# Masking a chunk's matrices as they leave PSUM, in the recurrence of a two-layer encoder: one VectorE instruction in place of a ScalarE copy and a GpSimd product

## The chip, the cores and the metric

The kernel runs on one core of one Trainium2 chip. The metric is the time of one execution on the device in microseconds (us), the median of several runs. The core's engines work in parallel, each through its own instructions in order: TensorE (PE in the profile, with PEld for its weight loads), VectorE (DVE), ScalarE (ACT), GpSimd (POOL) and the queue SP, which here issues nearly all DMAs. Matmul results land in PSUM, a small memory of eight banks per partition; everything else on the chip lies in SBUF.

## The reference: what is computed

A trunk of two layers on 1024 tokens of width 1024, all in float32. Layer 0 mixes tokens by dilated and windowed attention, layer 1 by a bidirectional recurrence; each layer ends with a squared-ReLU MLP of width 4096. The change lies in the recurrence of layer 1. For each of 16 heads (64 wide) and each of two directions the reference runs, token by token:

```python
def step(state, inp):
    r_t, w_t, k_t, v_t, kk_t, a_t = inp
    sa = jnp.einsum('bhvk,bhk->bhv', state, -kk_t)
    state = (state * w_t[:, :, None, :] + sa[..., None] * (kk_t * a_t)[:, :, None, :]
             + v_t[..., None] * k_t[:, :, None, :])
    return state, jnp.einsum('bhvk,bhk->bhv', state, r_t)
```

## The kernel before

The program is one stream: attention, MLP, the projections of the recurrence, the recurrence (`rwkv_scan`), the second MLP. The order of instructions on each engine is laid out at build time by the framework's planner from a simulated timeline with estimated durations (`schedule_with_timeline_sim=True`), within the data dependences and the priorities that the program gives. A change of an instruction's engine can therefore also change the order of its neighbours.

The recurrence is computed in chunks of 64 tokens. Heads are taken in eight batches (`Batch`), each with four steps (`G` counts all 32), and a step holds four pairs of heads and chunks for each of two directions `d`. Four generators do the work of a step:

- `prep` (lines 1240 to 1288) loads `x` and `rk`, takes exponentials on ScalarE (L1250, L1251), writes `zr` on VectorE (L1254, L1256) and `bk` half on VectorE (L1261) and half on GpSimd (L1262). Then, for `j` of 0 and 1, four matmuls (L1268) put a 128x512 block of the chunk's matrices into a PSUM tile, and the block goes to `af` in SBUF, multiplied by the triangular mask `amask`. These are the two instructions of the change, L1271 and L1272. After that `bk` is transposed (L1280) and copied to `bn` (L1282), and once both directions are done a part of `af` is written to `nd` in DRAM (L1286). `bk` is one buffer, so the next direction's L1261 and L1262 wait for the transposes. The PSUM tiles `A` of L1268 and L1280 come from a ring of two (`psA`).
- `invert` (lines 1290 to 1321) loads a batch's `nd` back as `nb` (L1294) and inverts its triangular blocks by thirty pairs of VectorE instructions, each needing the one before (L1300 and L1302), then sends the inverses through DRAM (`xd`) into `af`.
- `post` (from line 1323) completes the inverses for a step by small matmuls.
- `scan` (from line 1374) carries the states from chunk to chunk, with high priority: matmuls into `c`, evicted by ScalarE as `y` (L1395), the solved values `sv` copied by VectorE for one half (L1398) and by ScalarE for the other (L1399), the new state `h` written by ScalarE (L1407) and the output `ot` (L1418). After each of its pieces `side` puts in a piece of the generators above and of `finish` (group norm and gate, L1435 to L1447).

Before the first `scan` stands a prologue: `prep` of the first four steps, `invert` of the first batch, `post` of the first step, and `prep` of four steps more. From then on `prep` runs eight steps ahead of `scan`.

Of the kernel before, what the change touches and what calls it, by code (L numbers as in the profile page):

```python
# [9 lines left out]
AF = mybir.ActivationFunctionType  # L10
ALU = mybir.AluOpType
# [4 lines left out]
P = 128  # L16
# [9 lines left out]
def fsl(i, n):  # L26
    return slice(i * n, (i + 1) * n)
# [1115 lines left out]
def rwkv_scan(tc, g, ap, dr, yd):  # L1143
# [4 lines left out]
    nc = tc.nc  # L1148
    NS = T // P
    NX = 4 * (65 + 2 * RC)  # L1150
    with ExitStack() as es:
# [24 lines left out]
        consts = {}  # L1176
# [24 lines left out]
        def psa():  # L1201
            return psA.tile([P, 512], F32, tag="A", name="A")
# [7 lines left out]
        def c64(x):  # L1210
            return x.rearrange("p (c t) -> p c t", t=RC)

        def tokens(d, e, n):

            return slice(e * P, (e + n) * P) if d == 0 else slice((NS - e - n) * P, (NS - e) * P)

        def ordered(x, d):

            return (x if d == 0 else x[:, :, ::-1]).rearrange("p q (c t) -> p q c t", t=RC)

        def quad(x):
            return x.rearrange("p (q c) t -> p q c t", q=2)
# [11 lines left out]
        def prep(q, i):  # L1234

            e = 4 * q.half + i
            w = q.slots[i]
            sp = sl[(4 * q.b + i) % NQ]
            w.af = sp.tile([P, 2, 4, 2, P], F32, tag="af", name="af")
            w.zr, w.bn = ([sp.tile([P, 4, 2, RC], F32, tag=f"{n}{d}", name=f"{n}{d}") for d in range(2)] for n in ("zr", "bn"))  # L1240
            w.pc = [sp.tile([P, 4], F32, tag=f"pc{d}", name=f"pc{d}") for d in range(2)]
            for d in range(2):
                x = te.tile([P, NX], F32, tag="x", name="x")
                nc.sync.dma_start(out=x, in_=dr.x[d][q.m][:, e, :])
                rk = te.tile([P, 2, 2, P], F32, tag="rk", name="rk")
                nc.sync.dma_start(out=rk, in_=dr.rk[q.m][:, :, :, tokens(d, e, 1)])
                cs = x[:, 0:260].rearrange("p (q c t) -> p q c t", q=2, c=2)
                a, kd = (x[:, 260:].rearrange("p (q k c t) -> p q k c t", q=2, k=2, c=2)[:, :, k] for k in range(2))
                ipr = te.tile([P, 4, RC], F32, tag="ipr", name="ipr", bufs=1)
                nc.scalar.activation(quad(ipr), cs[..., 1:65], AF.Exp, scale=KAPPA)  # L1250
                nc.scalar.activation(cs, cs, AF.Exp, scale=-KAPPA)  # L1251
                nc.gpsimd.tensor_copy(w.pc[d].rearrange("p (q c) -> p q c", q=2), cs[..., 64])
                zr = w.zr[d]
                nc.vector.tensor_tensor(out=quad(zr[:, :, 0]), in0=cs[..., 0:64], in1=ordered(rk[:, :, 1], d),  # L1254
                                        op=ALU.mult)
                nc.vector.tensor_tensor(out=quad(zr[:, :, 1]), in0=cs[..., 1:65], in1=ordered(rk[:, :, 0], d),  # L1256
                                        op=ALU.mult)

                for j in range(2):
                    rows = fsl(j, 64)  # L1260
                    nc.vector.tensor_tensor(out=quad(bk[rows, :, j, j]), in0=kd[rows], in1=quad(ipr[rows]), op=ALU.mult)  # L1261
                    nc.gpsimd.tensor_tensor(out=quad(bk[rows, :, j, 1 - j]), in0=a[rows], in1=quad(ipr[rows]), op=ALU.mult)  # L1262
                yield

                for j in range(2):
                    ps = psa()
                    for u in range(4):
                        nc.tensor.matmul(ps[:, fsl(u, P)], lhsT=bk[:, u, j].rearrange("p a b -> p (a b)"),  # L1268
                                         rhs=zr[:, u].rearrange("p a b -> p (a b)"), start=True, stop=True)
                    o = w.af[:, d, :, j, :]  # L1270
                    nc.scalar.activation(o, ps.rearrange("p (u t) -> p u t", t=P), AF.Copy)  # L1271
                    nc.gpsimd.tensor_tensor(out=o, in0=o, in1=consts["amask"].unsqueeze(1).to_broadcast([P, 4, P]),  # L1272
                                            op=ALU.mult)
                    yield

                for j in range(2):
                    rows = fsl(j, 64)
                    ps = psa()
                    for u in range(4):
                        nc.tensor.transpose(ps[:, fsl(u, RC)], bk[rows, u, j].rearrange("p a b -> p (a b)"),  # L1280
                                            g.ident[rows, rows])
                    nc.scalar.activation(w.bn[d][:, :, j, :], c64(ps[:, 0:4 * RC]), AF.Copy)  # L1282
                if d == 1:
                    afv = w.af.rearrange("p d c j t -> p (d c) j t")
                    for j in range(2):
                        nc.sync.dma_start(out=q.nd[j, fsl(i, 8)].transpose([1, 0, 2]),  # L1286
                                          in_=afv[fsl(1 - j, 64), :, j, 0:64])
                yield
# [194 lines left out]
        for i in range(4):  # L1483
            b1.add(prep(bs[0], i))
# [7 lines left out]
        for G in range(4, NQ - 1):  # L1492
            if G % 4 == 0:
                bs.append(Batch(G // 4))
            b1.add(prep(bs[G // 4], G % 4))
# [3 lines left out]
        for G in range(4 * NB):  # L1499
# [10 lines left out]
            if g2 < 4 * NB:  # L1510
                if g2 % 4 == 0:
                    bs.append(Batch(g2 // 4))
                b1.add(prep(bs[g2 // 4], g2 % 4))
# [182 lines left out]
```

## Time and profile before

| what | us |
|---|---|
| median of 3 runs | 3607.05 |
| lowest and highest of them | 3602.4 and 3607.34 |
| the profiled execution | 3597.65 |
| its span, first to last instruction | 3595.9 |
| busy of that span: DVE | 2357.0 |
| busy: ACT | 1853.7 |
| busy: POOL | 1778.8 |
| first L1268, last L1268 (start) | 1890.6 and 2657.3 |
| first state copy L1398, last (start) | 2077.4 and 2791.0 |

Times inside the profile are counted from the span's start. The first layer and the projections fill the span up to about 1940; the prologue of the recurrence stands alone until about 2072; the recurrence proper runs to about 2800, and the second layer's output projection and MLP take the rest. A row of the timeline gives start, duration, engine, line, operation, the tile written and the tiles read; in square brackets is the idle time of the engine just before, and what ended it. A row of groups gives busy time and the mean of one instruction after the bar, then the engine's idle time in front of them.

### The profile page before, as it was taken

The numbers are of one execution on the slowest core, as the hardware profiler recorded it, in microseconds if no ns is written. First come the engines' busy times: TensorE is split into PE (matmuls) and PEld (weight loads), VectorE is DVE, ScalarE is ACT, GpSimd is POOL, SyncE is SP. The second block draws the span as 40 slices with busy tenths as digits, with TensorE's granted clock in tenths as the row PEclk, the third lists the DMA queues.
The fourth block names the chain that finished last, engine by engine and source line by source line (L and its number), as shares of the span: only waits on it lengthen the run. The fifth ranks groups of instructions, "written<-read, shape, count | busy, mean of one in ns | idle before, by whom it ended". The sixth has DMA issues, their size and how long they took to land. (4 is left out here: it accounts for less than half of the span.)

```text
span 3595.9 us, 61432 instructions
## 1 busy us (share of the span) xinstructions
PE 3213.8 (89%) x22616; PEld 2618.0 (73%) x22616; DVE 2357.0 (66%) x3917; ACT 1853.7 (52%) x4260; POOL 1778.8 (49%) x1606
## 2 busy tenths in 40 slices
PE   7999998899998897988888689899998989999988
PEld 6788896688876776666556577777776768877776
DVE  3455564654489987977964756766653474449996
ACT  2366564455543336764433366666667455554333
POOL 1000001465578886445557534445431265558887
PEclk9999999899999998999998589889899989999999
DMA  6222215143221323347776445455445322322113
GB/s 205 73 79 78 73 56 170 53 152 117 73 98 59 117 71 118 102 144 234 226 222 200 113 113 129 119 129 136 125 108 155 120 108 104 115 101 104 54 64 118
DMA packets 408203, 425.72 MB, mean 118 GB/s; under 512 B 138155, under 2 KB 321579, under 8 KB 401756
## 3 DMA queue, kind: packets, MB, share of 16 engines
q1 hardware_dynamic: 406716, 417.58, 37.1%
q0 software_dynamic: 1184, 4.20, 0.4%
q8 instruction: 178, 2.92, 0.3%
q14 instruction: 125, 1.02, 0.1%
HBM read 290.83 MB, written 138.20 MB: 119 GB/s over the span
## 5 line engine op out<-in xcount | busy, mean ns | idle before, releaser
L101 PE MATMUL pm<-bhi,lo 128*128 128x512 f32 x840 | 332.1, 398 | 47.8 <-DVE lo L130 47.6
L129 ACT ACTIVATE hi<-x 128x512 fp32r<-128x512 f32 x300 | 189.1, 631 | 340.8 <-DVE x L127 130.3
L130 DVE TENSOR_TENSOR lo<-x,hi 128x512 fp32r<-128x512 f32 x300 | 321.6, 1079 | 65.4 <-ACT hi L129 65.2
L100 PE MATMUL pm<-blo,hi 128*128 128x512 f32 x840 | 331.4, 395 | 8.4 <-POOL blo L130 7.9
L99 PE MATMUL pm<-bhi,hi 128*128 128x512 f32 x840 | 318.0, 395 | 6.2 <-ACT bhi L129 6.2
L127 POOL TENSOR_TENSOR x<-w1r 128x512 f32<-128x512 f32 x160 | 213.9, 1340 | 201.0 <-DVE lo L130 178.1
L130 POOL TENSOR_TENSOR blo<-bx,bhi 128x512 fp32r<-128x512 f32 x138 | 220.2, 1596 | 34.9 <-ACT bhi L129 34.4
L101 PEld LDWEIGHTS pm<-bhi,lo 128*128 128x128 f32 x840 | 157.9, 189 | 100.1 <-DVE lo L130 69.1
L1272 POOL TENSOR_TENSOR af<-af,amask 128x512 f32<-128x512 f32 x128 | 166.1, 1304 | 118.1 <-ACT af L1271 96.4
L905 POOL TENSOR_TENSOR wl<-wr,wh 128x512 fp32r<-128x512 f32 (+2 forms) x144 | 162.5, 1139 | 125.3 <-ACT wh L904 92.5
L1268 PE MATMUL A<-zr,bk 128*128 128x128 f32 x1024 | 181.1, 336 | 44.5 <-DVE bk L1261 40.1
L127 POOL TENSOR_TENSOR bx<-w 128x512 f32<-128x512 f32 x140 | 215.4, 1541 | 9.4
L127 DVE TENSOR_TENSOR x<-h 128x512 f32<-128x512 f32 x140 | 199.4, 1436 | 5.2 <-ACT h L268 2.7
L1268 PEld LDWEIGHTS A<-zr,bk 128*128 128x128 f32 x1024 | 158.5, 238 | 54.8 <-POOL af L1272 21.5
L100 PEld LDWEIGHTS pm<-blo,hi 128*128 128x128 f32 x840 | 158.4, 189 | 50.9 <-POOL blo L130 17.6
L99 PEld LDWEIGHTS pm<-bhi,hi 128*128 128x128 f32 x840 | 159.5, 190 | 39.9 <-ACT bhi L129 7.1
L99 PE MATMUL mm<-xmh,wh 128*128 128x512 f32 x384 | 164.1, 446 | 8.1 <-ACT wh L904 4.9
L1261 DVE TENSOR_TENSOR bk<-x,ipr 64x256 f32<-64x256 f32 x128 | 118.2, 924 | 70.8 <-PE A L1280 62.2
L1398 DVE COPY sv<-c 64x64 f32<-64x64 f32 x256 | 55.2, 226 | 163.9 <-PE c L1397 94.1
L583 ACT ACTIVATE S<-S,mneg 128x256 f32<-128x256 f32 (+2 forms) x256 | 124.6, 499 | 68.2 <-DVE mneg L578 45.3
L335 DVE TENSOR_TENSOR acc<-acc,pm 128x512 f32<-128x512 f32 x256 | 158.1, 674 | 0.0
L886 DVE SCALAR_TENSOR_TENSOR x<-u,mu,x 128x512 f32<-128x512 f32 x192 | 153.3, 831 | 7.2 <-ACT x L884 4.8
(368 smaller groups left out, 9936.7 us busy)
## 6 DMA issues: line engine op xcount, KB each, us to landing
w1r<-in_mlp_w_dram SPq DMA_DIRECT2D x32, 1024.0 KB, 5.6
w<-in_mlp_w_dram SPq DMA_DIRECT2D x32, 1024.0 KB, 5.2
x<-x SPq DMA_DIRECT2D x64, 386.0 KB, 3.5
hd<-h SPq DMA_DIRECT2D x24, 1024.0 KB, 4.2
h<-hd SPq DMA_DIRECT2D x24, 1024.0 KB, 7.8
wr<-in_w_rkv_dram SPq DMA_DIRECT2D x96, 256.0 KB, 2.9
x<-xo SPq DMA_DIRECT2D x32, 512.0 KB, 3.6
rk<-rk SPq DMA_DIRECT2D x64, 256.0 KB, 4.0
```

The source lines that it names most:

```text
L99: nc.tensor.matmul(out, lhsT=ahi, rhs=bhi, start=start, stop=False)
L100: nc.tensor.matmul(out, lhsT=ahi, rhs=blo, start=False, stop=False)
L101: nc.tensor.matmul(out, lhsT=alo, rhs=bhi, start=False, stop=stop)
L127: add.tensor_tensor(out=y, in0=x, in1=blocks[term[2]], op=ALU.add if term[1] == "+" else ALU.subtract)
L129: nc.scalar.activation(hi, x, AF.Copy)
L130: sub.tensor_tensor(out=lo, in0=x, in1=hi, op=ALU.subtract)
L335: dve.tensor_tensor(out=a, in0=a, in1=banks[j], op=ALU.add if sign == "+" else ALU.subtract)
L583: nc.scalar.activation(s[:, :n], s[:, :n], AF.Exp, bias=mneg[:, i:i + 1], scale=-1.0)
L886: nc.vector.scalar_tensor_tensor(out=x, in0=at(2 * i), scalar=mu[:, i, c, kt:kt + 1], in1=x, op0=ALU.mult, op1=ALU.add)
L905: nc.gpsimd.tensor_tensor(out=wlo, in0=wr, in1=whi, op=ALU.subtract)
L1268: nc.tensor.matmul(ps[:, fsl(u, P)], lhsT=bk[:, u, j].rearrange("p a b -> p (a b)"), rhs=zr[:, u].rearrange("p a b -> p (a b)"), start=Tru ...
L1272: nc.gpsimd.tensor_tensor(out=o, in0=o, in1=consts["amask"].unsqueeze(1).to_broadcast([P, 4, P]), op=ALU.mult)
```

## The change

In `prep`, the copy out of PSUM by ScalarE and the product with the mask in place by GpSimd become one product on VectorE, which reads the block from PSUM and the mask from SBUF and writes `af`. It runs once for each `j`, each direction and each of 32 steps: 128 times.

```diff
@@ -1268,9 +1268,8 @@
                         nc.tensor.matmul(ps[:, fsl(u, P)], lhsT=bk[:, u, j].rearrange("p a b -> p (a b)"),
                                          rhs=zr[:, u].rearrange("p a b -> p (a b)"), start=True, stop=True)
                     o = w.af[:, d, :, j, :]
-                    nc.scalar.activation(o, ps.rearrange("p (u t) -> p u t", t=P), AF.Copy)
-                    nc.gpsimd.tensor_tensor(out=o, in0=o, in1=consts["amask"].unsqueeze(1).to_broadcast([P, 4, P]),
-                                            op=ALU.mult)
+                    mask = consts["amask"].unsqueeze(1).to_broadcast([P, 4, P])
+                    nc.vector.tensor_tensor(out=o, in0=ps.rearrange("p (u t) -> p u t", t=P), in1=mask, op=ALU.mult)
                     yield
```

## The prediction, made before the changed kernel was run

> **What bounds the kernel now.** I read the page first, then the busy times by stage, the timeline of the prologue, and the waits of the recurrence. The page has TensorE as the fullest engine, but the share is a mean over stages:
>
> ```profile
> PE 3213.8 (89%) x22616; PEld 2618.0 (73%) x22616; DVE 2357.0 (66%) x3917; ACT 1853.7 (52%) x4260; POOL 1778.8 (49%) x1606
> ```
>
> The busy times by stage (start and end, length, busy of each engine with its count, granted clock, DMA share) part the stretch that holds all of L1271 and L1272 into prologue (first three rows; the second is the inverse of the first batch), recurrence with `prep` beside it, and recurrence alone:
>
> ```profile
> core 0: us, PE busy (x) PEld busy (x) DVE busy (x) ACT busy (x) POOL busy (x), PEclk, DMA share, GB/s
> 1943.00:2003.00 60.00, 40.05 (x224) 35.91 (x224) 37.89 (x38) 24.34 (x55) 43.45 (x52) 0.65 0.57 148
> 2003.00:2053.40 50.40, 30.32 (x152) 27.44 (x153) 46.99 (x86) 15.91 (x36) 27.42 (x32) 0.64 0.36 98
> 2053.40:2100.00 46.60, 30.59 (x444) 26.48 (x444) 27.88 (x75) 21.68 (x66) 12.23 (x17) 0.67 0.41 88
> 2100.00:2660.00 560.00, 521.20 (x7944) 425.83 (x7944) 347.26 (x757) 364.39 (x1204) 266.43 (x322) 0.90 0.51 128
> 2660.00:2830.00 170.00, 147.83 (x2396) 117.55 (x2397) 74.21 (x189) 107.56 (x362) 29.08 (x40) 0.94 0.46 129
> ```
>
> In the prologue nothing is full except DVE during the inverse (46.99 of 50.40); in the recurrence PE is at 521.2 of 560, with 38.8 us idle. So the prologue is a loop bound by latency, and the timeline shows the loop. One turn, in order of time:
>
> ```profile
> 1965.99 0.91 POOL L1262 TENSOR_TENSOR bk<-x,ipr 64x256 f32<-64x256 f32 x1
> 1966.23 3.03 DVE L1261 TENSOR_TENSOR bk<-x,ipr 64x256 f32<-64x256 f32 x2
> 1966.86 1.25 POOL L1272 TENSOR_TENSOR af<-af,amask 128x512 f32<-128x512 f32 x1
> 1968.19 0.79 POOL L1262 TENSOR_TENSOR bk<-x,ipr 64x256 f32<-64x256 f32 x1
> 1968.54 3.40 PE L1268 MATMUL A<-zr,bk 128*128 128x128 f32 x16 [2.34 <-DVE bk L1261]
> 1970.62 0.60 ACT L1271 ACTIVATE af<-A 128x512 f32<-128x512 f32 x1 [0.86 <-PE A L1268]
> 1971.97 0.60 ACT L1271 ACTIVATE af<-A 128x512 f32<-128x512 f32 x1 [0.45 <-PE A L1268]
> 1972.63 0.46 PE L1280 MATMUL A<-ident,bk 64*128 64x64 f32 x4 [0.30 <-ACT af L1271]
> 1973.16 3.03 DVE L1261 TENSOR_TENSOR bk<-x,ipr 64x256 f32<-64x256 f32 x2
> ```
>
> The turn from `bk` to `bk` takes 1973.16 - 1966.23 = 6.93 us: `bk` written, two matmul groups, two evictions, transposes, `bk` again. Of it 3.03 us are the two L1261. They end at 1969.26, 0.28 us after GpSimd's second L1262 (1968.98), and that one stands behind L1272. How long L1261 takes unhindered is seen in the line views (minimum, median, maximum in ns):
>
> ```profile
> L1261 DVE TENSOR_TENSOR bk<-x,ipr x128: 406/829/2931, 1887.9 to 2654.7; 64x256 f32<-64x256 f32 x128
> L1272 POOL TENSOR_TENSOR af<-af,amask x128: 1251/1270/1854, 1899.1 to 2658.7; 128x512 f32<-128x512 f32 x128
> L1271 ACT ACTIVATE af<-A x128: 570/597/619, 1896.9 to 2657.6; 128x512 f32<-128x512 f32 x128
> L335 DVE TENSOR_TENSOR acc<-acc,pm x256: 670/674/677, 1036.4 to 3543.6; 128x512 f32<-128x512 f32 x128
> ```
>
> Two L1261 would be 0.81 us. They are stretched whenever a GpSimd product lies beside them; I read this as GpSimd holding back a VectorE instruction that reads two SBUF tiles. L335, a VectorE product of the same size with one input in PSUM, varies by only 7 ns, though the MLPs keep GpSimd busy beside it. It is the nearest row to the new instruction.
>
> **The change part by part.** Removed: 128 L1271 by 597 ns = 76.4 us of ScalarE, and 128 L1272, 166.1 us of GpSimd by the page. Added: 128 VectorE products; I take L335's 674 ns, so 86.3 us. The mask is read with a repeated axis, which no row shows beside a PSUM input; bounds are 0.6 us (the ScalarE eviction) and 1.27 us (the GpSimd product), and I take the row of the same engine and shape. The dependences stay: matmul, masked block, then the transposes' PSUM tile and the store of `nd`. No DMA is added.
>
> Term A, the turns ahead of the first inverse. In a turn, L1272 goes from between the two L1262. The second L1262 then starts right behind the first and ends at 1966.90 + 0.08 + 0.79 = 1967.77 in place of 1968.98: 1.21 us sooner, and L1261 ends behind it as now. The second eviction costs 0.674 in place of 0.597: +0.08. VectorE is in order, and must now fit mask, `zr` and mask between its `bk`s. `zr` is two instructions of about 0.42 us; between the two masks it fills the time of the second matmul group (1971.97 - 1970.62 = 1.35 us) and 0.67 + 0.84 = 1.51 overhangs by about 0.15. That is -1.21 + 0.08 + 0.15 = -0.98 us a turn. The inverse begins behind the `bk` of 2000.88:
>
> ```profile
> 1945.50 3.02 DVE L1261 TENSOR_TENSOR bk<-x,ipr 64x256 f32<-64x256 f32 x2
> 2000.88 2.15 DVE L1261 TENSOR_TENSOR bk<-x,ipr 64x256 f32<-64x256 f32 x1
> 2002.96 0.70 DVE L1300 TENSOR_TENSOR xtmp<-nb 128x30 f32<-128x30 f32 x1
> 2053.21 0.19 DVE L1302 TENSOR_TENSOR nb<-nb,xtmp 128x30 f32<-128x30 f32 x1
> 1988.91 0.58 SPq L1286 DMA_DIRECT2D nd<-af  x1
> 1991.59 2.11 SPq L1294 DMA_DIRECT2D nb<-nd  x2
> ```
>
> Eight turns lie between those two `bk` (55.4 us / 6.93), so 8 x 0.98 = 7.8, and 1.2 for the last `bk` itself: **A = -9.0**. The data come as early: the last store of `nd` (1988.91) moves with seven turns and with a block that is ready 2 us sooner (0.67 in place of 0.60 and 1.25 in two queues). If the plan puts VectorE's pieces otherwise, A may be -2 (rivals) or at best 9 x 1.25 = -11.
>
> Term B, the inverse itself (2002.96 to 2053.40), where VectorE is full and everything it loses or gains shows:
>
> ```profile
> L1272 POOL TENSOR_TENSOR af<-af,amask 128x512 f32<-128x512 f32 x12 | 15.5, 1288 | 19.8 <-ACT af L1271 14.2 <-issue 5.6
> ```
>
> Twelve L1272 of 15.5 us together stand in VectorE's way there; twelve masks bring 12 x 0.674 = 8.1. **B = -7**, a little under the difference of 7.4. Bounds: -15.5 if the masks fell into VectorE's gaps (there are 3.4 us, so hardly), +8.1 if nothing were given back.
>
> From the end of the inverse to the first state (2053 to 2077) come DMA round trips with few masks: 0. They move forward as a whole.
>
> Term C, the recurrence, 2100 to 2660, with 92 masks. The waits of PE and DVE there (total, times, longest), and the groups:
>
> ```profile
> PE c L1402 <- ACT sv L1399: 26.8, 19, 3.7
> PE c L1410 <- ACT sv L1399: 2.0, 1, 2.0
> DVE sv L1398 <- PE c L1397: 66.6, 46, 5.4
> DVE sv L1398 <- ACT af L1271: 12.8, 5, 4.2
> L1271 ACT ACTIVATE af<-A 128x512 f32<-128x512 f32 x92 | 53.0, 590 | 19.4 <-PE A L1268 10.2 <-PE c L1410 7.0 <-DMA x<-x 0.8
> L1272 POOL TENSOR_TENSOR af<-af,amask 128x512 f32<-128x512 f32 x92 | 119.9, 1312 | 78.3 <-ACT af L1271 64.6 <-DMA af<-xd 6.1 <-ACT ot L1418 6.0
> L1261 DVE TENSOR_TENSOR bk<-x,ipr 64x256 f32<-64x256 f32 x90 | 76.4, 849 | 26.3 <-PE A L1280 21.9 <-ACT y L1395 2.0 <-ACT h L1407 0.5
> ```
>
> Most of PE's 38.8 us of idle time, 28.8 of it, is waiting for the state's copies: `sv` L1399, which follows L1398 on VectorE. ScalarE loses 53.0 us that stood in line with four of the scan's evictions (L1395, L1399, L1407, L1418); VectorE, which has one of them (L1398), gets 92 x 0.674 = 62.0 us. It gets something back: L1261 alone lose 90 x (849 - 406) = 39.9 us there, and L1272 with its 119.9 us is the longest GpSimd work beside them; I put half, 20 us, and as much for the rest of VectorE's two-tile products, both estimates. VectorE ends near 347 + 62 - 40 = 369 of 560 us, not full. The one row that ties a removed instruction to the scan is 12.8 us in which L1398 waited until an L1271 had gone. I take half of it as PE time: **C = -6**, between 0 (PE stays the bound, the waits come back on VectorE) and -28.8 (all these waits go); above zero in the rival.
>
> Sum: -9 - 7 + 0 - 6 = **-22 us**. On the profiled execution (3597.65, of which 3595.9 is span and 1.75 lies around it) that gives 3575.6. The median of the runs shown is 9.4 us above the profiled one; taken from the median, 3607.05 - 22 = **3585 us**.
>
> A rule that speaks against the change: the Trainium skill, page Perfetto Trace Analysis, section Optimizing Scalar/DVE Operations, says that where VectorE is saturated it may make sense to hand work to ScalarE or even GpSimd; this edit does the reverse. By that rule term B would be a loss. The trace bears it out only for that one stretch, and there the row of L1272 speaks for the hindrance being the larger part. It is the last of the rivals.
>
> **The rivals.** *More than forecast.* The state's copies come free: C = -20, sum -36, 3571 us. And the clock: the two matmul groups of a turn took 3.40 us at a low granted clock. Compare these stretches, and a group of eight on the chain of waits later on:
>
> ```profile
> 1910.00:1920.00 10.00, 10.00 (x53) 8.23 (x52) 0.79 (x1) 5.68 (x10) 9.09 (x8) 1.00 0.80 278
> 1990.00:2000.00 10.00, 8.13 (x40) 7.33 (x40) 4.42 (x6) 4.01 (x9) 5.36 (x6) 0.50 0.85 171
> 2429.84 1.09 PE A L1268 x8
> ```
>
> With PE full the clock is 1.00, in the loop with its gap of 2.34 us it is 0.50, and 16 matmul records would take 2.18 us at the speed of the last row. If the shorter turn raised the clock, eight turns would gain 8 x 1.2 = 10 us more. The Trainium skill, page TensorE: Matmul & The Clock Gate, section Part 1 (What's actually happening), has the clock at half after an idle window of about 3.4 us and at full after a busy one. By that rule the loop, whose gap shrinks but stays, could go either way; the forecast keeps the clock. I give this rival 0.17, with times of 3555 to 3577.
>
> *No change, by order.* The planner puts `zr` behind the second mask: then 0.84 us stand on the turn's path, the turn gains -1.21 + 0.08 + 0.84 = -0.29, A = -2.3. In the inverse each mask waits on VectorE for its matmuls, as ScalarE did (0.86 and 0.45 us before the two L1271 quoted); 12 x 0.65 = 7.8 cancels B. C = 0. Sum about -2, 3605 us. For it: VectorE already stands 2.3 us a turn waiting for a ScalarE result; against: those waits lie where the masks would go. 0.15.
>
> *Slower, by the state's copy.* A mask stands on VectorE ahead of L1398 and waits for its matmul group, which PE holds behind the scan's own. The copy waits, ScalarE's L1399 behind it, the next state's matmuls L1402 behind that. Price of one case: at most 1.09 for the group and 0.67 for the mask, 1.76 us. It cancels A and B (16 us) from 9 full cases in 92 masks on; with 20 cases C = +35 and the sum is +19, 3626 us. For it: L1398 waits 66.6 us for PE already, and L1268 is placed by an estimate. Against: ScalarE's L1271 waited only 19.4 us in 92 cases, on an engine with four times as many of the scan's evictions. 0.11.
>
> *Slower, by a full VectorE.* If VectorE's long L1261 come from something else than L1272 (the two L1262 suffice to hold it), nothing is given back: A = 8 x (0.08 + 0.15) = +1.8, B = +8.1, C = 0, sum +10, 3617 us. Against it: L1261 ends behind the GpSimd product whatever its own length. 0.06. That the change doesn't do what it says is hardly open: two instructions go, one comes.
>
> **How the numbers follow.** Forecast (sum of -8 to -30, so 3577 to 3599): 0.51. With the rivals above: faster by over 0.2% (7.2 us) 0.51 + 0.17 = 0.68; within 0.2% 0.15; slower 0.11 + 0.06 = 0.17. The three runs lie within 0.14% of one another, so 0.2% is about what a measurement of this kernel can tell from no change. The range goes down to 3558, leaving out a small part of the larger gain (0.03), and up to 3617, which takes in no change and the full VectorE and leaves out the copy's delay (0.11).
>
> **What would show it.** Right: the turn in the prologue falls from 6.93 to about 6 us; the two L1261 from 3.03 to about 1.8; masks on VectorE at 670 to 680 ns each, with no tail; the inverse from 50.4 to about 43 us; the first L1398 at 2077.4 - 16 = 2061; the stretch from there to the last L1398 (713.6 us) shorter by about 6. Wrong: masks over 0.8 us; L1261 unchanged in median (A and B fall); `zr` behind both masks; L1402's wait for L1399 above 28 us, or L1398 waiting for L1268 (the slower rival). What would make the number wrong with every step right is a new order on PE or SP's queue, which the planner draws anew for everything from 1890 on.

## The result, and the profile after

The changed kernel took 3551.23 us in the median (3549.82 to 3553.83 in 4 runs) against 3607.2 us (3602.4 to 3612.86 in 4 runs) for the kernel before: 56 us less, a ratio of 0.9845 with a 95% interval of 0.9828 to 0.9862. The forecast was 3585 us in a range of 3558 to 3617: the sign was right, the gain two and a half times the one forecast.

Below line 1271 the changed file has one line less, so L1299 and L1301 are the inverse's products that were L1300 and L1302, L1397 and L1398 the two copies of `sv`, L1401 the state's matmuls that were L1402, L1279 the transposes. L1272 is now VectorE's mask.

Two profiles of each kernel give the stages (the second ones come from the section "The stages again"). The stretches end at the starts of the rows named:

| stretch | before | after |
|---|---|---|
| start to the first L1268 | 1890.7, 1892.2 | 1892.8, 1900.3 |
| to the first product of the inverse | 112.3, 110.8 | 95.4, 93.3 |
| to the first copy of `sv` by VectorE | 74.4, 73.7 | 67.5, 67.4 |
| to the last such copy | 713.6, 723.9 | 690.6, 691.1 |
| to the end | 804.9, 804.4 | 805.7, 804.7 |

On their means the first inverse begins 17.2 us sooner, the way from there to the first state loses 6.6 us, and the recurrence 27.9 us, 51.7 us in sum. What follows the recurrence is as long as before; the stretch ahead of the first L1268 is 0.6 to 9.6 us longer in the profiles after, which nothing here explains. The first profile of the kernel before (3597.65 us) was one of its quickest executions; in later groups of runs it spread from 3591.61 to 3616.91 us.

The busy times by stage of the changed kernel, with the columns of the prediction's table; the last two rows part the recurrence where `prep` ends:

```profile
1946.00:1988.00 42.00, 32.00 (x230) 28.10 (x231) 30.67 (x56) 15.36 (x38) 22.14 (x35) 0.84 0.77 203
1988.00:2036.80 48.80, 31.49 (x189) 27.52 (x187) 46.05 (x107) 13.68 (x34) 15.50 (x24) 0.73 0.51 142
2036.80:2055.70 18.90, 6.59 (x128) 6.00 (x128) 3.32 (x13) 4.53 (x10) 1.44 (x3) 0.52 0.67 118
2055.70:2603.00 547.30, 518.05 (x8202) 419.82 (x8203) 352.35 (x904) 336.06 (x1152) 151.58 (x235) 0.94 0.52 131
2603.00:2746.30 143.30, 124.27 (x2272) 99.69 (x2272) 61.80 (x168) 96.65 (x333) 19.86 (x28) 0.88 0.45 123
```

and the same two stretches of the recurrence in the kernel before:

```profile
2077.40:2657.00 579.60, 534.01 (x8165) 436.71 (x8166) 365.87 (x812) 375.15 (x1240) 265.42 (x325) 0.89 0.50 125
2657.00:2791.00 134.00, 117.37 (x2308) 93.66 (x2306) 61.02 (x169) 95.82 (x340) 24.24 (x31) 0.95 0.48 132
```

With practically the same count of matmul records, the stretch with `prep` is 32.3 us shorter: TensorE is busy 16.0 us less, its clock at 0.94 in place of 0.89, and idles 16.3 us less. Then 9.3 us are given back where `prep` has ended: 6.9 us of it are busy time of TensorE at a clock of 0.88 in place of 0.95, and 2.4 us are idle time. (In the second pair of profiles the two figures are 40.8 us and 8.0 us, cut in the same way.) The way of the last batch's inverse through DRAM is on the chain of waits of the changed kernel, first two rows, but just as long on that of the kernel before, last two rows, so it does not explain the 9.3 us; their cause stays open:

```profile
2604.29 4.03 DMA nd<-af
2609.03 5.41 DMA nb<-nd
2661.22 3.33 DMA nd<-af
2665.21 5.55 DMA nb<-nd
```

The prologue's timeline, VectorE's masks and two rows beside them, with the clock of two stretches of 10 us:

```profile
1956.66 0.69 DVE L1272 TENSOR_TENSOR af<-A,amask 128x512 f32<-128x512 f32 x1 [0.62 <-PE A L1268]
1962.81 0.69 DVE L1272 TENSOR_TENSOR af<-A,amask 128x512 f32<-128x512 f32 x1 [1.36 <-PE A L1268]
1968.30 0.69 DVE L1272 TENSOR_TENSOR af<-A,amask 128x512 f32<-128x512 f32 x1 [1.58 <-PE A L1268]
1976.48 0.69 DVE L1272 TENSOR_TENSOR af<-A,amask 128x512 f32<-128x512 f32 x1 [0.31 <-PE A L1268]
1978.43 1.49 DVE L1261 TENSOR_TENSOR bk<-x,ipr 64x256 f32<-64x256 f32 x2
1979.07 2.13 PE L1268 MATMUL A<-zr,bk 128*128 128x128 f32 x16 [0.30 <-DVE bk L1261]
1980.23 0.69 DVE L1272 TENSOR_TENSOR af<-A,amask 128x512 f32<-128x512 f32 x1 [0.31 <-PE A L1268]
1960.00:1970.00 10.00, 8.80 (x42) 8.10 (x43) 5.61 (x12) 2.66 (x7) 3.33 (x6) 0.51 0.51 145
1970.00:1980.00 10.00, 7.69 (x64) 6.64 (x64) 9.21 (x15) 3.98 (x10) 5.11 (x8) 1.00 0.71 185
```

The first masks of successive turns stand 6.15 and 5.49 us apart at a clock of 0.51, where the forecast had about 6. From 1970 the clock is 1.00 and a turn takes 1980.23 - 1976.48 = 3.75 us: the 16 matmul records of a turn have fallen from 3.40 to 2.13 us, and in front of them TensorE idles 0.30 us where it idled 2.34.

### The profile page after: what moved, and what is told of

It is laid out like the page before. It is cut to its first block, busy times and chain, and to the rows that moved or that the text cites. A ratio compares the mean times of both kernels' runs of the same rounds, so it can differ in the third digit from the quotient of the medians.

```text
span 3552.0 us, 61192 instructions
## 1 busy us (share of the span) xinstructions
PE 3185.9 (90%) x22616; PEld 2588.5 (73%) x22616; DVE 2333.9 (66%) x4045; ACT 1797.9 (51%) x4132; POOL 1611.2 (45%) x1478
## 5 line engine op out<-in xcount | busy, mean ns | idle before, releaser
L1262 POOL TENSOR_TENSOR bk<-x,ipr 64x256 f32<-64x256 f32 x128 | 108.9, 851 | 201.2 <-PE A L1279 137.6
L1268 PE MATMUL A<-zr,bk 128*128 128x128 f32 x1024 | 166.0, 312 | 14.7 <-DVE bk L1261 8.8
L1268 PEld LDWEIGHTS A<-zr,bk 128*128 128x128 f32 x1024 | 141.1, 213 | 25.2 <-POOL bk L1262 10.6
L100 PE MATMUL mm<-xml,wh 128*128 128x512 f32 x384 | 154.1, 401 | 0.5 <-DVE xml L891 0.5
L101 PE MATMUL mm<-xmh,wl 128*128 128x512 f32 x384 | 144.4, 401 | 0.0
```

The lines of the kernel that those rows point to most:

```text
L100: nc.tensor.matmul(out, lhsT=ahi, rhs=blo, start=False, stop=False)
L101: nc.tensor.matmul(out, lhsT=alo, rhs=bhi, start=False, stop=stop)
```

## The experiments

Each was timed beside the kernel before; ratios are to that kernel in the same group of runs. For comparison, the changed kernel has 0.9845.

**Where the gain sits: one stage at a time.** The mask by VectorE in the first eight steps of `prep` alone, then in all others alone:

```diff
-                    nc.vector.tensor_tensor(out=o, in0=ps.rearrange("p (u t) -> p u t", t=P), in1=mask, op=ALU.mult)
+                    if 4 * q.b + i < 8:   # the second kernel: >= 8
+                        nc.vector.tensor_tensor(out=o, in0=ps.rearrange("p (u t) -> p u t", t=P), in1=mask, op=ALU.mult)
+                    else:
+                        nc.scalar.activation(o, ps.rearrange("p (u t) -> p u t", t=P), AF.Copy)
+                        nc.gpsimd.tensor_tensor(out=o, in0=o, in1=mask, op=ALU.mult)
```

> The new mask in the first eight steps of prep only (those of the prologue), the old pair of instructions in the rest. If the two stages gain independently: the first state copy comes 19 to 22 us sooner, the recurrence keeps its 713 us, time about 3585 us (3578 to 3592). Rival, that the later gain hangs on the new order set up in the prologue: the recurrence shortens too, time under 3570.

> The old pair in the first eight steps, the new mask from the ninth step on. If the stages gain independently: the prologue as in the kernel before (first state copy at 2075 to 2080), the recurrence some 23 to 34 us shorter, time about 3573 to 3584 us. Rival, that the recurrence shortened only because it began with more steps prepared: time above 3595.

Measured: 3590.44 us, ratio 0.9952 (0.9938 to 0.9967), with the prologue alone; 3576.2 us, 0.993 (0.9908 to 0.9952), with the rest alone. From the first L1268 to the first copy of `sv` it is 165.4 us with the prologue's masks and 186.2 us without (before 184.5 and 186.7); the recurrence takes 730.5 us and 687.7 us. So each stage keeps a gain of its own, and the gain of about 20 us in the prologue is partly given back: there the old recurrence behind it is 7 to 17 us longer than in the two profiles of before. The two gains, 16 and 30 us, add up to 46 of the 56; where the other 10 come from was not tried.

**Which engine's relief is it?** First GpSimd's product is put back beside the new mask, into a scratch tile that nobody reads; then ScalarE keeps the eviction and VectorE masks from SBUF:

```diff
                     nc.vector.tensor_tensor(out=o, in0=ps.rearrange("p (u t) -> p u t", t=P), in1=mask, op=ALU.mult)
+                    nc.gpsimd.tensor_tensor(out=scr, in0=o, in1=mask, op=ALU.mult)
```
```diff
-                    nc.vector.tensor_tensor(out=o, in0=ps.rearrange("p (u t) -> p u t", t=P), in1=mask, op=ALU.mult)
+                    nc.scalar.activation(o, ps.rearrange("p (u t) -> p u t", t=P), AF.Copy)
+                    nc.vector.tensor_tensor(out=o, in0=o, in1=mask, op=ALU.mult)
```

> The changed kernel, and behind each new mask a GpSimd product of the masked block with the mask into a scratch tile that nobody reads: GpSimd's load is back, ScalarE stays relieved, VectorE keeps the mask. If the gain is GpSimd no longer holding back VectorE's products of two SBUF tiles: the median of L1261 goes back from 0.42 to about 0.8 us, the time goes back to 3595 to 3620 us. Rival, that the gain is ScalarE's shorter queue ahead of the state's copies and the shorter chain in prep: time stays at 3550 to 3562 us.

> The eviction by ScalarE as before, then the mask in place by VectorE from SBUF: GpSimd is relieved, ScalarE is not. If GpSimd's hindrance of VectorE was the cost: most of the gain stays, 3553 to 3570 us, with L1261 near 0.45 us in median and masks that are now themselves stretched beside L1262. Rival, ScalarE's queue: PE's wait for the sv copies goes back above 20 us and the time to 3580 to 3600 us.

Measured: with the product back 3608.55 us, 1.0005 (0.9991 to 1.002): the whole gain is gone although ScalarE stays relieved. The median of `bk` by VectorE did not go back (423 ns), against what I expected; the loss shows in the means of the recurrence: 643 ns for `bk` where the changed kernel has 540, 455 and 445 ns for the inverse's products where it has 375. VectorE carries the masks here and is held as well, so this run does not price GpSimd's product alone. With ScalarE's eviction kept 3579.8 us, 0.9933 (0.9914 to 0.9951): half of the gain, at the lower edge of what the rival gave. Its masks in the stretch with `prep`, and TensorE's wait over the whole recurrence:

```profile
L1273 DVE TENSOR_TENSOR af<-af,amask 128x512 f32<-128x512 f32 x91 | 69.9, 775 | 34.9 <-ACT af L1272 34.0 <-issue 0.2
PE c L1402 <- ACT sv L1399: 18.6, 18, 2.8
```

The mask from SBUF takes 775 ns on average against 690 from PSUM. TensorE's wait is 18.6 us; over the same stretch it is 30.6 us in the kernel before, 7.9 in the changed kernel and 28.6 with the product put back. So about half of this wait goes when GpSimd no longer reads, and the other half only when ScalarE's copy goes as well. ScalarE's queue, the longer way out of PSUM and the masks that are now held themselves are the candidates for that other half; they were not tried one by one.

**Does GpSimd hold VectorE by being busy or by reading?** The first of these fills a scratch tile for as long as the old product took, the second multiplies a scratch tile in place and waits for nothing:

```diff
+                    nc.gpsimd.memset(scr, 0.0)
+                    nc.gpsimd.memset(scr, 0.0)
+                    nc.gpsimd.memset(scr[:, 0:256], 0.0)
```
```diff
+                    nc.gpsimd.tensor_tensor(out=scr, in0=scr, in1=mask, op=ALU.mult)
```

> The changed kernel, and beside each new mask GpSimd fills a scratch tile with zeros for about 1.3 us (two fills of 128x512 and one of 128x256): GpSimd is as busy as before, but reads nothing. If the cost of GpSimd's product was that it holds back VectorE's products of two SBUF tiles by reading SBUF: time stays within 10 us of the changed kernel (3551 to 3562) and the inverse's L1299 near 375 ns in the recurrence. Rival, that GpSimd's own queue (L1262 behind it) was the cost: time back to 3590 us or more.

> The changed kernel, and beside each new mask a GpSimd product of a scratch tile with the mask, in place, that waits for nothing and that nobody reads: the fill's kernel with a product of two SBUF tiles in place of the fills. If GpSimd's reading of SBUF holds back VectorE: time 3585 to 3612 us, the inverse's products in the recurrence at 440 to 490 ns in place of 375. Rival, that the dependent product brought the time back only because it reads the masked block and so holds it longer: 3545 to 3560 us, as with the fills.

Measured: with the fills 3545.3 us, 0.985 (0.982 to 0.9879), no different from the changed kernel; with the product 3618.99 us, 1.0035 (1.0021 to 1.0049), above the range that I expected. The inverse's products, first with fills (2057 to 2590), then with the product (2076 to 2673), and `bk` by VectorE over the whole span in the latter (minimum, median, maximum):

```profile
L1303 DVE TENSOR_TENSOR xtmp<-nb 128x150 f32<-128x150 f32 (+9 forms) x175 | 65.9, 377 | 13.7 <-DMA nb<-nd 9.1
L1305 DVE TENSOR_TENSOR nb<-nb,xtmp 128x130 f32<-128x130 f32 (+4 forms) x176 | 64.3, 365 | 4.4
```
```profile
L1302 DVE TENSOR_TENSOR xtmp<-nb 128x30 f32<-128x30 f32 (+9 forms) x180 | 78.5, 436 | 19.6 <-DMA nb<-nd 14.2 <-issue 0.9
L1304 DVE TENSOR_TENSOR nb<-nb,xtmp 128x30 f32<-128x30 f32 (+9 forms) x180 | 76.8, 427 | 5.1
L1263 DVE TENSOR_TENSOR bk<-x,ipr x128: 404/422/6977, 1892.4 to 2661.7; 64x256 f32<-64x256 f32 x128
```

The planner did not leave the added work beside the masks. It depends on nothing, so all fills were done by 2213 and all products by 2232, in the prologue and the start of the recurrence. The two runs can still be compared, since both have their added work in the same place. From the first matmul of the chunk's matrices to the first state it is 165.1 us with the fills and 203.8 us with the products (18.0 us of it TensorE's waits for a GpSimd that was busy with them), and the recurrence takes 672.9 and 705.7 us. From 2101 to 2232, beside the products, the inverse's two products take 505 and 508 ns on average; from there to 2667, without them, 405 and 378. So in these runs a GpSimd busy with fills costs nothing, and a GpSimd that reads SBUF holds VectorE's products of two SBUF tiles. Why the recurrence is longer beyond 2232 as well is not shown; its clock is 0.91 with the products and 0.96 with the fills. One `bk` of 0.4 us took 6.98 us, at 1924.76, while GpSimd went through products almost without a gap (of the added ones, of `wl` and of `y`). The Trainium skill, page SBUF — State Buffer, section Who interferes with whom, has this rule: a VectorE instruction with two SBUF inputs contends with a GpSimd instruction that reads SBUF, not with one that only writes it. The pair of runs agrees with both halves.

**The clock.** Matmuls into a free PSUM tile at the end of each turn of the prologue, whose product is not used: three a turn in the kernel before, two a turn in the changed kernel, later one a turn in the kernel before:

```diff
+                if 4 * q.b + i < 8:
+                    pw = psl()
+                    for _ in range(3):   # 2 in the changed kernel; 1 in the last
+                        nc.tensor.matmul(pw, lhsT=consts["ones64"], rhs=scr, start=True, stop=True)
```

> The kernel before, with three more matmuls of 128x512 at the end of each turn of the prologue (first eight steps of prep), into a PSUM tile that is free there; their product is not used. If TensorE's granted clock is low in the prologue because TensorE idles in each turn, and the turn is long in part because of the clock: granted clock above 0.85 from 1960 to 2050, and the first state copy comes 5 to 15 us sooner after the first L1268 in spite of the added 1.8 us a turn. Rival, that the clock follows something else: the clock stays at 0.5 to 0.7 and the prologue grows by 15 to 50 us.

> The changed kernel, with two more such matmuls at the end of each turn of the prologue, not used. If the clock still costs there: clock near 1.0 throughout the prologue and the time 2 to 8 us shorter than the changed kernel's, 3543 to 3549 us. Rival, that VectorE and the DMA round trips set the prologue by now: 3551 to 3565 us.

> The kernel before, with one added matmul of 128x512 (its product is not used) a turn of the prologue; three of them took 5.6 us a turn and held the clock at 1.00, so one takes about 1.9 us, which fits the 2.3 us that TensorE idles in a turn. If the low clock is a cost of its own: clock above 0.85 from 1946 to 2003, a turn of 5.6 to 6.2 us in place of 6.93, the first state copy 5 to 12 us sooner after the first L1268 than 184.5 to 186.7 us, so 173 to 181. Rival, that the turn is set by GpSimd and VectorE and the clock only follows: the turn stays at 6.9 us or above and the first copy at 184 us or later.

Measured: 3610.37 us, 1.0027 (1.001 to 1.0043); 3567.98 us, 0.9912 (0.9880 to 0.9944); 3609.47 us, 1.0017 (0.9999 to 1.0035). None gains, and the first state came later in each of the three: 198.9, 177.6 and 192.2 us after the first matmul of the chunk's matrices, where the kernel before has 184.5 to 186.7 and the changed kernel 160.7 to 162.9. I had expected it sooner in the kernel before. I had the added matmuls at 0.6 us each, and three of them took 5.6 us of a turn. But they show the clock. With three a turn it was 1.00 from 1946 to 2003, with TensorE never idle:

```profile
1946.00:2003.00 57.00, 57.00 (x281) 33.55 (x280) 21.23 (x32) 19.70 (x46) 38.33 (x44) 1.00 0.47 139
```

With one a turn, the planner put the added matmuls ahead of 1976 only, and the same execution has one turn at full clock and then turns at half clock behind them, with no added matmul in them. `bk` by VectorE (now L1263) and the matmul groups (L1270):

```profile
1976.82 0.59 DVE L1263 TENSOR_TENSOR bk<-x,ipr 64x256 f32<-64x256 f32 x1 [0.82 <-PE A L1282]
1980.14 1.16 PE L1270 MATMUL A<-zr,bk 128*128 128x128 f32 x8 [0.94 <-POOL bk L1264]
1981.98 3.03 DVE L1263 TENSOR_TENSOR bk<-x,ipr 64x256 f32<-64x256 f32 x2
1988.91 3.03 DVE L1263 TENSOR_TENSOR bk<-x,ipr 64x256 f32<-64x256 f32 x2
1991.22 3.76 PE L1270 MATMUL A<-zr,bk 128*128 128x128 f32 x16 [1.81 <-DVE bk L1263]
1995.85 3.03 DVE L1263 TENSOR_TENSOR bk<-x,ipr 64x256 f32<-64x256 f32 x2
```

A group of eight records takes 1.16 us in the turn that begins at 1976.82, and that turn lasts 5.16 us. A few microseconds on, sixteen records take 3.76 us and a turn lasts 6.93 us, the length that it had in the kernel before. So this one turn at full clock was 6.93 - 5.16 = 1.77 us shorter, with GpSimd's products still there; its two `bk` took 0.59 and 1.92 us in place of 3.03 together, and whether that goes with the clock is not shown. In the changed kernel the same step is 5.49 - 3.75 = 1.74 us (from the second of its turns at the low clock; the first took 6.15). Read the other way, the change itself takes 1.44 us from a turn at the low clock and 1.41 at full clock. A clock that was high in only a part of the turn brought nothing here: the kernel before ran three turns at a mean clock of 0.75 and later two at 0.50, and all five took 6.93 us (busy times as in the prediction's table):

```profile
1954.67:1975.47 20.80, 12.89 (x73) 11.79 (x73) 13.32 (x13) 7.99 (x19) 15.44 (x20) 0.75 0.39 108
1982.39:1996.25 13.86, 10.12 (x48) 8.98 (x49) 8.31 (x9) 5.38 (x12) 8.86 (x11) 0.50 0.66 138
```

The Trainium skill, page TensorE: Matmul & The Clock Gate, section Part 1 (What's actually happening), lets recent activity decide the clock; that agrees with the filled loop at 1.00.

**What is left of GpSimd's reading.** The other half of `bk` (L1262) to VectorE as well, on top of the change; the same in the kernel before; and, on top of the first, the sum `y` of `finish`:

```diff
-                    nc.gpsimd.tensor_tensor(out=quad(bk[rows, :, j, 1 - j]), in0=a[rows], in1=quad(ipr[rows]), op=ALU.mult)
+                    nc.vector.tensor_tensor(out=quad(bk[rows, :, j, 1 - j]), in0=a[rows], in1=quad(ipr[rows]), op=ALU.mult)
```
```diff
-            nc.gpsimd.tensor_tensor(out=y, in0=y, in1=gt, op=ALU.add)
+            nc.vector.tensor_tensor(out=y, in0=y, in1=gt, op=ALU.add)
```

> The changed kernel, and the other half of bk (L1262, 128 products of 64x256) moved from GpSimd to VectorE too. If what GpSimd still holds back is worth more than the added 128 x 0.42 = 54 us of VectorE: 3535 to 3550 us. Rival, that VectorE becomes the bound in prologue and recurrence: 3555 to 3580 us.

> The kernel before (mask by ScalarE and GpSimd), with the other half of bk (L1262) on VectorE. L1262 is 1.6 us of GpSimd a turn against L1272's 2.5. If each GpSimd product costs by the time that it holds VectorE: a gain of 20 to 35 us, as L1262 brought on top of the change, so 3570 to 3587 us. Rival, that L1262 is cheap as long as L1272 stands beside it: 3595 us or more.

> The version with mask and both halves of bk on VectorE, and the sum y of finish (32 GpSimd products of 128x512) on VectorE as well: GpSimd keeps only fills and small copies. If what GpSimd reads still costs: 3510 to 3520 us. Rival, that VectorE's added 32 x 0.69 = 22 us now show: 3528 to 3545 us.

Measured: 3524.55 us, 0.9787 (0.9763 to 0.9812), for `bk` on top of the change: the fastest version, 78.7 us below the kernel before of its group where the change alone has 56.0. 3532.79 us, 0.9791 (0.9767 to 0.9814), with `y` too: no further gain, against what I expected; what GpSimd stopped reading and what VectorE took on were not priced apart. And 3641.49 us, 1.0089 (1.006 to 1.0117), for `bk` in the kernel before, a loss of 34 us where I expected a gain. The groups of `bk` in the recurrence, with the change and without it, and the latter's busy times:

```profile
L1262 DVE TENSOR_TENSOR bk<-x,ipr 64x256 f32<-64x256 f32 x90 | 40.1, 445 | 0.1
L1261 DVE TENSOR_TENSOR bk<-x,ipr 64x256 f32<-64x256 f32 x90 | 39.9, 444 | 33.0 <-PE A L1279 29.1 <-PE B L1354 1.2 <-ACT h L1406 1.0
```
```profile
L1261 DVE TENSOR_TENSOR bk<-x,ipr 64x256 f32<-64x256 f32 x88 | 58.0, 659 | 38.9 <-PE A L1280 21.4 <-ACT h L1407 10.5 <-ACT y L1395 3.4
L1262 DVE TENSOR_TENSOR bk<-x,ipr 64x256 f32<-64x256 f32 x88 | 47.0, 534 | 0.0
2076.00:2680.00 604.00, 557.55 (x8022) 450.86 (x8019) 372.43 (x891) 367.06 (x1214) 190.13 (x231) 0.84 0.47 119
```

With the mask still on GpSimd both halves of `bk` on VectorE are held (659 and 534 ns in place of 444 and 445), and the clock is at 0.84. The loss lies in the recurrence, which takes 756.0 us in place of 713.6 to 723.9; the first state comes 187.6 us after the first L1268, hardly later than before. What makes the whole 34 us was not tried; VectorE is not full there (372 of 604 us), and TensorE idles 46.5 us, about as in the kernel before, so the clock is the suspect and no more.

**The stages again.** The second profiles, in the table above:

> The kernel before, a second profile. If stages repeat: first L1268 to first state copy 186 to 188 us, first to last state copy 708 to 720 us. If the recurrence's length differs by more than 10 us between executions of one kernel, the sizes read from single profiles are that uncertain.

> The changed kernel, a second profile. If stages repeat: first L1268 to first state copy 162 to 164 us, first to last state copy 680 to 698 us.

Measured: 184.5 and 723.9 us before, 160.7 and 691.1 us after; three of the four lie 1.3 to 3.9 us outside what I expected. The recurrence of the kernel before differs by 10 us between two executions, so its gain of 27.9 us is known to some 5 us.

## Why the prediction was right in sign and wrong in size

**The mask's cost: right.** 674 ns with no tail was forecast. All 128 masks over the span, in ns:

```profile
L1272 DVE TENSOR_TENSOR af<-A,amask x128: 678/691/693, 1902.0 to 2603.0; 128x512 f32<-128x512 f32 x128
```

**Term A, -9 forecast, -17.2 measured.** Two L1261 fell from 3.03 us to 1.8, as forecast, and at full clock to 1.49. The turn at the low clock lost 1.44 us in place of 0.98: the overhang of mask and `zr` that I had added (0.15 us) did not show, and the other 0.31 us are not accounted for. At the low clock VectorE is done with `zr` before TensorE's second group ends, and waits 0.35 us for it:

```profile
1964.52 0.69 DVE L1272 TENSOR_TENSOR af<-A,amask 128x512 f32<-128x512 f32 x1 [0.35 <-PE A L1268]
```

The step that failed is another: "the forecast keeps the clock". In the turn from 1960.73 to 1966.19, still at half clock, TensorE was busy 4.99 of 5.46 us, where the loop of before at half clock has 10.12 of 13.86; behind it the clock rose, and the turns from 1970 on lost 1.74 us more. That the smaller idle share raised the clock is inferred; the filled loop, never idle and at 1.00, agrees. The case was among the rivals, with 10 us for eight turns. The prediction's picture of the clock was itself misread: the turn that it quotes, with the gap of 2.34 us and 3.40 us of matmul records, ran at a mixed clock (0.75 on average over three such turns), while the 0.50 is that of later turns, with a gap of 1.80 us and 3.75 us of records.

**Term B, -7 forecast, and 0 behind it.** The inverse took 48.6 us in place of 50.4, only 1.8 less, with more of `prep` in the same stretch: sixteen masks where twelve were counted, and 17 L1261 where there were 14:

```profile
L1272 DVE TENSOR_TENSOR af<-A,amask 128x512 f32<-128x512 f32 x16 | 11.0, 687 | 0.7 <-PE A L1268 0.5
```

The `prep` that was done there was missing afterwards: from the end of the inverse to the first state it is 18.9 us in place of 24.0. Together -6.9 us in the first pair of profiles. That this equals the forecast is luck: most of it fell in the stretch that the forecast put at nothing.

**Term C, -6 forecast, -27.9 measured.** The mechanism was the one named, the copies of `sv`; the size was wrong in two ways. The waits of TensorE in the stretch with `prep`, first the row of before that the prediction did not show, then the changed kernel's:

```profile
PE c L1404 <- ACT sv L1399: 3.6, 4, 1.8
```
```profile
PE c L1401 <- ACT sv L1398: 5.7, 9, 1.5
PE c L1403 <- ACT sv L1398: 2.1, 3, 1.5
```

From 26.8 + 3.6 + 2.0 = 32.4 us they fell to 7.8; 8.3 of these 24.6 us came back as other idle time of TensorE. The step of the prediction that failed is the size of this term: I had tied only 12.8 us of VectorE's waits to the change and taken half. What I left out is the inverse, which stands in VectorE's queue ahead of the copies. It is not all of the rest: where VectorE masked from SBUF, the inverse's products were nearly as short as here (386 and 376 ns) and 16.6 of the 32.4 us were still there; these went only when ScalarE's eviction went too. The inverse's products in that stretch, before and after:

```profile
L1302 DVE TENSOR_TENSOR nb<-nb,xtmp 128x150 f32<-128x150 f32 (+9 forms) x175 | 85.4, 488 | 5.0
L1300 DVE TENSOR_TENSOR xtmp<-nb 128x168 f32<-128x168 f32 (+9 forms) x174 | 80.3, 461 | 25.6 <-DMA nb<-nd 20.6
```
```profile
L1301 DVE TENSOR_TENSOR nb<-nb,xtmp 128x150 f32<-128x150 f32 (+9 forms) x175 | 65.7, 375 | 4.6
L1299 DVE TENSOR_TENSOR xtmp<-nb 128x168 f32<-128x168 f32 (+9 forms) x174 | 65.2, 375 | 18.8 <-DMA nb<-nd 14.6
L1261 DVE TENSOR_TENSOR bk<-x,ipr 64x256 f32<-64x256 f32 x90 | 48.6, 540 | 35.2 <-PE A L1279 29.5 <-ACT y L1394 2.4 <-ACT h L1406 1.4
```

They give back 34.8 us and L1261 27.8, 62.6 us in sum; I had put 40 for all of VectorE. The masks cost 62.2 us, so VectorE pays for them out of what it was held. The second part of the miss is the clock again, which the sum of term C did not have: 0.94 for 0.89, 16 us of TensorE's busy time. That the clock rose because the waits went is inferred from the prologue's runs; in the recurrence it was not tried by itself.

**The rivals.** No change by order, and VectorE too full, did not come about. The delay of the state's copy did not decide: VectorE did wait 37.0 us in front of masks in the recurrence (26.2 for L1268, 10.8 for the scan's L1409), yet TensorE's wait for the copies fell. The larger gain was named with its two causes and given 0.17; its times ended at 3555, 4 us above what was measured, since each cause was put in for one stage alone.

## What to carry to other kernels

In this kernel GpSimd's products, which read SBUF, cost VectorE time even where GpSimd had plenty to spare: count every VectorE product of two SBUF tiles that runs beside it, not only the one next to it, before calling GpSimd's work free. The masks that read PSUM were not held in this way (690 ns on average, even beside the product put back), and the 62.2 us that they added to VectorE in the recurrence came back from what it was no longer held. That does not make every such move a gain: moving `bk` won 22 us more once the mask was on VectorE and lost 34 us while it was on GpSimd. Where TensorE waits in each turn of a loop, price the turn at both clocks, and reckon with a shortened loop changing from one to the other.

## What was not expected of the hardware

One and the same loop ran a turn of 5.16 us at full clock and, right behind it in the same execution, turns of 6.93 us at half clock; yet 6.93 us is also what it took at a mean clock of 0.75. And a VectorE product of 0.4 us can be held for 6.98 us by a train of GpSimd products.
